# A hybrid attention and recurrence layer: the forget sums and the memory's second tile one step earlier, and eight block copies ahead of panel 12

## The chip, the cores and the metric

The kernel runs on one core of one Trainium2 chip. The metric is the device time of one execution in microseconds. Three runs of the kernel before took 755.61, 753.70 and 755.33 us, with a median of 755.33.

## What is computed

One layer for 512 tokens of width 1024, in float32: a combined input projection, forgetting attention with 8 heads of 64 (FoX), a gated linear recurrence with 4 heads (HGRN2), an output projection, cross attention to 256 memory tokens, a squared-ReLU MLP of width 4096 and a final norm. Cut to what bears on the change:

```python
hn = rmsnorm(h, norm_mix_g)
fq, fk, fv, ff, gq, gf, gi, gg = split(hn @ w_in)
log_f = log_sigmoid(ff + fox_f_bias)
F = cumsum(log_f, axis=-1)                       # per head over the tokens
s = einsum('bhqd,bhkd->bhqk', q, k) / 8 + F[:, :, :, None] - F[:, :, None, :]
fox = softmax(where(causal, s, -inf)) @ v
rec = hgrn2_chunkwise(gq, gf, gi, lb)            # state S_t = diag(f_t) S_{t-1} + k_t i_t^T
rec = rmsnorm(rec, hgrn_norm_g) * silu(gg)
h = h + concat(fox, rec) @ w_out
mem_n = rmsnorm(mem, norm_mem_g)
h = h + memory_cross_attention(rmsnorm(h, norm_x_g), mem_n, w_xq, w_xkv, w_xo)
u = rmsnorm(h, norm_ff_g) @ w1
h = h + square(relu(u)) @ w2
return rmsnorm(h, final_norm_g)
```

## The kernel before

All products run on PE in float32 of high and low parts: an operand is split into hi (ACT, `wh...`, L184) and lo = raw − hi (DVE, `wl...`, L188), and three matmuls make a product. The weights stream through as panels 0 to 28 or so; a panel's raw tiles `wr...` are loaded on SP's queue, in two halves a and b (L210). Panels 5 to 11 are the seven products of a block scheme (`product_unit`, L264), in which block sums take the place of single blocks. Some of their operands are made by loads on POOL's queue that accumulate into the tile: `third_sum` (L256, four tiles `wrs`, used by the splits wh9, wl9) and `fourth_sum` (L260, wrs6a and wrs6b, used by wh11, wl11). Panels 12, 13 and 15 are attention queries and keys of head pairs, 14 attention values, 16 and more belong to the memory and the projections behind.

The MLP far behind uses the same scheme with block sums that are made in DRAM beforehand. For each sum a **block copy** (`first`, L496: 512 KB of a weight block from DRAM to DRAM scratch, tiles `wsu` and `wsd`) goes out on SP's queue, and later an accumulating load on POOL's queue adds the other block (L507). The copies wait in a list, `copies`. `load_unit` takes so many of them behind each part of a panel as the table `COPIES` says for the panel's number (L215), and the projection panels take more from 24 on. `keep_in_program_order` fixes their place on SP's queue. There are 45 copies in all.

Around the change PE runs the recurrence's output in four steps c = 0 to 3 of 128 tokens each (L1064 and on), and fills the time between them with matmuls of the attention's projections (`fill`). A step:
- PE makes po; ACT squares it (`hj`, L1093); POOL turns the sums into the norm's factor (`hr...e`, L435, and `hr`, L438); DVE scales it (`rec`, L1097).
- PE transposes `rec` of the step before (`pr`, L1046); ACT and DVE write it as `mx_hi` (L1047) and `mx_lo` (L1048).

Two pieces of preparation for what follows hang on these steps by the numbers `MT, NF = 3, 2`:
- At c == NF, `fox_rows(0)` (L1023) broadcasts the forget sums F of the first two heads from DRAM (`Fd`) to all 128 partitions: two tiles `nF` of 256 KB, loaded on POOL's queue (L1026).
- At c == MT, `load_mem(1)` (L1030) loads the memory's second tile of 128 tokens (`mt`, POOL's queue, L1032) and normalises it: two squares on ACT (`m1j`, L445), their sum on DVE (`m1m`, L446), the factor on POOL (`m1re`, L435, `m1r`, L438), the scaling on DVE (`mt`, L448).

Behind the recurrence comes the attention of the first pair. POOL makes the biases from nF (`bi`, L1165, with the causal mask, L1166); PE the scores `ps` (L1174); DVE adds the bias and takes the maximum (L1185); ACT the exponential (L1187); DVE the reciprocal `dn` and the product (L1188, L1189). PE then transposes the probabilities (`pt`, L1201), which DVE and ACT copy (`pts`). A scheduler orders each engine's instructions ahead of time by priorities; each engine works through its own list in that order.

Of the kernel before, what the change touches and what calls it, by code (L numbers as in the profile page):

```python
# [30 lines left out]
GF = 5  # L31
WARM, WARM2 = 7, 4
P1, P2, P3, P4, PW = 20, 20, 20, 10, -20
MT, NF = 3, 2
F1, F2, F3, F4, B1 = 1.6, 3.2, 1.5, 1.0, 2.0

FX = (4.4, 4.4, 5.4, 5.4), (3.3, 3.9, 4.5, 5.1)
# [1 line left out]
NEG = -3.0e38  # L39
SEVEN = (1, 2, 3, 4, 5, 6, 7)  # L40
RAWS, HB, LOADS = 5, 4, 8
COPIES = {12: 2, 14: 3, 17: 2, 19: 1, 20: 0, 24: 1}
PACE = (178.0, 4.7), (301.0, 11.5)


# [1 line left out]
def emit(  # L47
# [61 lines left out]
    def t2(name, dt=F32, shape=(S,)):  # L109
        return t2p.tile([P] + list(shape), dt, tag="t2", name=name)  # L110
# [12 lines left out]
    def sc(name, shape=(S,)):  # L123
        return scp.tile([P] + list(shape), F32, tag="sc", name=name)
# [24 lines left out]
    def block0(rc):  # L149
        r, c = int(rc[0]), int(rc[1])  # L150
        return w_in[r * S : (r + 1) * S, 2568 + c * S : 2568 + (c + 1) * S].rearrange("(k p) n -> p k n", p=P)
# [19 lines left out]
    copies, copied = deque(), set()  # L171
    UW, UK = WT + FH, KC // 2

    def new_parts(shape, name):
        pad = [P, UK * (UW + FH)]
        hi = whp.tile([P, shape[0] * shape[1]], R, tag="wh", name=f"wh{name}", padded_shape=pad)
        lo = wlp.tile([P, shape[0] * shape[1]], R, tag="wl", name=f"wl{name}", padded_shape=pad)
        return [t.rearrange("p (k n) -> p k n", k=shape[0]) for t in (hi, lo)]

    def split_of(hi, lo, raw):  # L180
        def split(what="hl"):
            at = None
            if "h" in what:
                at = ac.activation(hi, raw, AF.Copy)  # L184
            if "v" in what:
                ve.tensor_copy(hi, raw)
            if "l" in what:
                at_lo = ve.tensor_tensor(lo, raw, f(hi), ALU.subtract)  # L188
                return at or at_lo
            return at  # L190

        return split

    def load_unit(name, spec, ks, parts=1, between=None):
# [12 lines left out]
        for q in range(parts):  # L207
# [5 lines left out]
            if between is not None:  # L213
                between(q)
            for _ in range(next((n for at, n in reversed(COPIES.items()) if len(stream) >= at), 0)):  # L215
                if copies:
# [4 lines left out]
    def load_next(parts=2, between=None):  # L221

        i = len(stream)
        if i >= len(specs):
            return []
        if callable(specs[i]):
            return specs[i]()
        units, splits = [], []
        uk = specs[i][0][1].shape[1] // 2
        for n in range(2):  # L230
            note = None if between is None else (lambda q, n=n: between(n * parts // 2 + q))
            unit, some = load_unit(f"{i}{'ab'[n]}", specs[i], slice(n * uk, (n + 1) * uk), parts // 2, note)
            units.append(unit)
            splits += some
        stream.append(tuple([u[x] for u in units] for x in range(2)))
        return splits
# [3 lines left out]
    def load_block(name, rc, tiles):  # L240
        raw0[name] = tiles
        for u, t in enumerate(tiles):
            tc.keep_in_program_order(nc.sync.dma_start(t, block0(rc)[:, 2 * u : 2 * u + 2, :]))
# [20 lines left out]
    def product_unit(name):  # L264
        parts = [new_parts([2, S], f"{len(stream)}{u}") for u in "ab"]
        stream.append(tuple([u[x] for u in parts] for x in range(2)))
        if name in "13":
            pad = [P, UK * UW]
            tiles = [wrp.tile([P, 2 * S], F32, tag="wr", name=f"wr0{name}{u}", padded_shape=pad) for u in "ab"]
            load_block(name, "00" if name == "1" else "11", [t.rearrange("p (k n) -> p k n", k=2) for t in tiles])  # L270
        if name == "1":
            for k in range(4):
                t = q2p.tile([P, S], F32, tag="q2", name=f"wrs7{k}")
                tc.keep_in_program_order(nc.sync.dma_start(t, block0("01")[:, k, :]))
                sums7.append(t)
        jobs = []
        for u in range(2):
            hi, lo = parts[u]
            if name == "7":
                jobs += [split_of(hi[:, k, :], lo[:, k, :], sums7[2 * u + k]) for k in range(2)]  # L280
                continue
            raw = raw0[{"2": "5", "4": "6"}.get(name, name)][u]
            jobs.append(split_of(hi, lo, raw))
        if name == "3":
            jobs.append(fourth_sum)
        if name == "3":
            jobs.append(lambda: load_block("5", "10", raw0["5"]))
        return jobs
# [60 lines left out]
    def ahead(n):  # L349

        return tc.high_priority(offset=n) if n else nullcontext()
# [217 lines left out]
    def x_park(c):  # L569
        part, dst = c // 2, park[:, c, :]  # L570
        if c % 2 == 0:
            ac.activation(dst, xps[c], AF.Copy)
        else:
            ve.tensor_copy(dst, xps[c])
        parked.add(c)
        if c ^ 1 in parked:
            gp.dma_start(xTd[part], park[:, 2 * part : 2 * part + 2, :])

    def x_sq(tb):
        junk = s4([D], f"x0j{tb}")  # L580
        if tb < 2:
            ac.activation(junk, xt[:, tb, :], AF.Square, scale=1.0 / 32.0, accum_out=ms0[:, tb : tb + 1])
        else:
            ve.tensor_tensor_reduce(out=junk, in0=xt[:, tb, :], in1=xt[:, tb, :], scale=1.0 / D, scalar=0.0, op0=ALU.mult, op1=ALU.add, accum_out=ms0[:, tb : tb + 1])
# [4 lines left out]
    with tc.manual_schedule(engines={mybir.EngineType.Activation, mybir.EngineType.DVE}):  # L589
# [26 lines left out]
        def l_soft():  # L616
# [12 lines left out]
        jobs = (  # L629
            (first[1],),  # L630
            (lambda: x_park(0), lambda: x_park(1), first[2]),
            (first[3], lambda: second.extend(load_next())),
            (lambda: x_sq(0), lambda: x_park(3)),
            (lambda: x_park(2), lambda: second[0]("h"), lambda: x_sq(2)),
            (lambda: x_sq(1), lambda: second[0]("l"), lambda: x_sq(3)),
            (lambda: second[1]("hl"), l_soft),
            (),
# [47 lines left out]
        def qt_(h):  # L685
            return (Mv, Sa)[h % 2][h // 2][:, h % 2, :]
# [336 lines left out]
    def fox_rows(p):  # L1023
        for h in (2 * p, 2 * p + 1):
            fF[h] = t2(f"nF{h}")
            gp.dma_start(fF[h], Fd[h, :].partition_broadcast(P))  # L1026
# [37 lines left out]
    for c in range(NT):  # L1064
        cs = slice(c * P, (c + 1) * P)
        it = iv[c // 2][:, c % 2, :].rearrange("p (h v) -> p h v", v=P)
        gt = gg[c // 2][:, c % 2, :].rearrange("p (h v) -> p h v", v=P)
        po = sc(f"po{c}", (4, P))
        for h in range(4):
            te.matmul(po[:, h, :], Ag[h // 2][:, (h % 2) * 4 + c, :], it[:, h, :], start=True, stop=c == 0)  # L1070
            if c > 0:
                te.matmul(po[:, h, :], qt_(h)[:, cs], St[:, h, :], start=False, stop=True)
        if c < NT - 1:
            pst = sc(f"pst{c}", (4, P))
            for h in range(4):
                te.matmul(pst[:, h, :], kts[c][:, h, :], it[:, h, :], start=True, stop=True)
            if c < NT - 2:
                k_T(c + 1)
            with ahead(P2):
                Sn = t2(f"S{c}", F32, (4, P))  # L1080
                if c == 0:
                    ve.tensor_copy(Sn, pst)
                else:
                    for h in range(4):
                        ve.scalar_tensor_tensor(
                            Sn[:, h, :], St[:, h, :], Fg[h // 2][:, h % 2, c * P : c * P + 1], pst[:, h, :], op0=ALU.mult, op1=ALU.add
                        )
                St = Sn
        with ahead(P1):
            hs = sm(4, f"hs{c}")  # L1090
            for h in range(4):
                j = t2(f"hj{c}{h}", F32, (P,))
                ac.activation(j, po[:, h, :], AF.Square, scale=128.0 ** -0.5, accum_out=hs[:, h : h + 1])  # L1093
            hr = rstd_of(hs, 4, f"hr{c}")
            rec = t2(f"rec{c}", F32, (4, P))
            for h in range(4):
                ve.scalar_tensor_tensor(rec[:, h, :], po[:, h, :], hr[:, h : h + 1], gt[:, h, :], op0=ALU.mult, op1=ALU.mult)  # L1097
        fill.run(H1)
        if c == NT - 2:
            fill.until("proj0")  # L1100
        if c == MT:
            load_mem(1)
        if c == NF:
            fox_rows(0)
        if pending is not None:
            to_mix(*pending)
        pending = (c, rec)
        fill.run(H2)
# [839 lines left out]
    with tc.manual_schedule(engines={mybir.EngineType.Activation, mybir.EngineType.DVE}):  # L1948
        c = KC - 1
# [105 lines left out]
```

## Time and profile before

| | value |
|---|---|
| runs | 755.61, 753.70, 755.33 us (median 755.33) |
| the profiled execution's own time | 754.02 us |
| its span | 752.2 us |
| mean granted clock of PE | 0.993 |
| PE busy | 740.2 us (98%) |
| DVE busy | 565.5 us (75%) |
| ACT busy | 460.4 us (61%) |
| POOL busy | 212.5 us (28%) |
| DMA moved | 159.22 MB, mean 212 GB/s |

The span is the time between the first and the last instruction in the trace; the execution's own time lies 1.8 us over it. All times in what follows are counted from the start of the span. In a row of the timeline stand the start, the busy time, the engine, the line, the operation, out<-in, the shapes, and in brackets how long the engine had idled before, and for what. A "q" behind an engine's name means the queue of its DMA issues. The chapters on stretches (windows) give busy time per engine, then PE's granted clock, the mean busy share of the 16 DMA engines and GB/s.

### The profile page before, as it was taken

To read this page: it belongs to the slowest core of one execution; us is meant where nothing else is said; L and a number is where in the kernel's file an instruction comes from. 1 tells how busy PE (TensorE), PEld (TensorE's weight loads), DVE (VectorE), ACT (ScalarE), POOL (GpSimd) and SP (SyncE) were. 2 spreads that over 40 slices of the span, in tenths; PEclk is the share of its full clock that TensorE was granted. 3 is DMA by queue.
4 is the path that set the end of the run, shared out by engine and by line. 5 is a ranking of instruction groups with operands and counts; after the bars stand their busy time and mean duration, and the time that the engine had idled before them with its cause. 6 is when DMAs were issued, how large, how long until landed. Compare 5 with 4: busy or idle time off the path is not lost.

```text
span 752.2 us, 12313 instructions
## 1 busy us (share of the span) xinstructions
PE 740.2 (98%) x4557; PEld 646.4 (86%) x4557; DVE 565.5 (75%) x892; ACT 460.4 (61%) x769; POOL 212.5 (28%) x290
## 2 busy tenths in 40 slices
PE   9999999979999999999999999999999999999996
PEld 6889888878888888888888899898989899999985
DVE  5876996656788856645555798978788787878796
ACT  5965776545666642334444589666576757574864
POOL 8225842332433227721111212111111111100034
PEclk9999999989999999999999999999999999999999
DMA  7787859948856799987579799998989898977452
GB/s 228 261 215 196 195 142 341 341 146 291 275 201 213 259 273 220 186 169 135 115 167 203 106 251 229 247 224 244 229 214 240 222 246 211 245 195 233 132 112 112
DMA packets 111919, 159.22 MB, mean 212 GB/s; under 512 B 6338, under 2 KB 74219, under 8 KB 111859
## 3 DMA queue, kind: packets, MB, share of 16 engines
q1 hardware_dynamic: 85490, 114.62, 46.9%
q0 software_dynamic: 26208, 43.54, 33.0%
q8 instruction: 36, 0.59, 0.3%
q10 hardware_dynamic: 160, 0.27, 0.1%
q14 instruction: 25, 0.20, 0.1%
HBM read 153.15 MB, written 51.40 MB: 272 GB/s over the span
## 4 chain that ended last, share of the span: by engine, by line
PE 88%; DMA 4%; ACT 3%; DVE 2%; issue 1%; POOL 1%; POOLq 0%; DVEq 0%; SPq 0%; ACTq 0%
PE uU L1630 4%; PE uU L1632 4%; PE uU L1631 4%; PE U L1789 4%; PE U L1788 4%; PE U L1790 4%; PE uY L1632 2%; PE uY L1631 2%; PE uY L1630 2%; PE xk L1144 2%; PE xq L314 2%; PE wo L314 2%; PE xq L315 2%; PE xw L314 2%; PE xq L316 2%; PE xw L316 2%
## 5 line engine op out<-in xcount | busy, mean ns | idle before, releaser
L188 DVE TENSOR_TENSOR wlu<-wru,whu 128x1024 fp32r<-128x1024 f32 x53 | 63.8, 1221 | 25.6 <-ACT whu L184 25.6
L184 ACT ACTIVATE whu<-wru 128x1024 fp32r<-128x1024 f32 x53 | 55.6, 1058 | 40.9 <-PE U L1790 16.8
L188 DVE TENSOR_TENSOR wld<-wrd,whd 128x1024 fp32r<-128x1024 f32 x56 | 68.2, 1221 | 13.8 <-ACT whd L184 13.5
L184 ACT ACTIVATE whd<-wrd 128x1024 fp32r<-128x1024 f32 x56 | 59.0, 1054 | 15.2 <-PE uU L1631 7.1
L1788 PE MATMUL U<-whd,hb 128*128 128x512 f32 x120 | 46.8, 390 | 0.0
L1789 PE MATMUL U<-wld,hb 128*128 128x512 f32 x120 | 46.8, 390 | 0.0
L1790 PE MATMUL U<-whd,hb 128*128 128x512 f32 x120 | 46.7, 389 | 0.0
L1165 POOL TENSOR_SCALAR bi<-nF,Ft 128x128 f32<-128x128 f32 (+3 forms) x32 | 20.7, 654 | 63.5 <-PE pt L1201 27.6
L507 POOL DMA_DIRECT2D wsd<-in_w_dram x16 | 17.8, 1114 | 68.2 <-PE xw L316 16.6
L1630 PE MATMUL uU<-xs_hi,whu 128*128 128x256 f32 x128 | 36.3, 284 | 0.0
L1632 PE MATMUL uU<-x_hi,wlu 128*128 128x256 f32 x128 | 36.2, 283 | 0.0
L1630 PE MATMUL uY<-xs_hi,whu 128*128 128x256 f32 x128 | 36.2, 283 | 0.0
L1631 PE MATMUL uY<-xs_lo,whu 128*128 128x256 f32 x128 | 36.2, 283 | 0.0
L1632 PE MATMUL uY<-xs_hi,wlu 128*128 128x256 f32 x128 | 36.2, 283 | 0.0
L1632 PE MATMUL uU<-xs_hi,wlu 128*128 128x256 f32 x128 | 36.2, 283 | 0.0
L1631 PE MATMUL uU<-x_lo,whu 128*128 128x256 f32 x128 | 36.2, 283 | 0.0
L1631 PE MATMUL uU<-xs_lo,whu 128*128 128x256 f32 x128 | 36.2, 283 | 0.0
L1630 PE MATMUL uU<-x_hi,whu 128*128 128x256 f32 x128 | 36.2, 283 | 0.0
L1526 POOL DMA_DIRECT2D wrd<-in_w_dram x8 | 9.8, 1223 | 86.6 <-DVE wld L188 59.6
L507 POOL DMA_DIRECT2D wsu<-in_w_dram x14 | 16.9, 1210 | 44.3 <-PE xq L316 14.5
L1187 ACT ACTIVATE bi<-bi,mx 128x128 f32<-128x128 f32 (+3 forms) x32 | 17.9, 559 | 18.4 <-DVE mx L1185 17.4
L1790 PEld LDWEIGHTS U<-whd,hb 128*128 128x128 f32 x120 | 22.5, 188 | 4.7
(1012 smaller groups left out, 2650.9 us busy)
## 6 DMA issues: line engine op xcount, KB each, us to landing
wru<-in_w_dram SPq DMA_DIRECT2D x25, 512.0 KB, 6.7
wsd<-in_w_dram SPq DMA_DIRECT2D x24, 512.0 KB, 8.5
wrd<-in_w_dram SPq DMA_DIRECT2D x24, 512.0 KB, 4.1
wrd<-wsd SPq DMA_DIRECT2D x24, 512.0 KB, 5.3
wsu<-in_w_dram SPq DMA_DIRECT2D x21, 512.0 KB, 7.0
wru<-wsu SPq DMA_DIRECT2D x21, 512.0 KB, 4.8
wsd<-in_w_dram POOLq DMA_DIRECT2D x16, 512.0 KB, 7.9
wsu<-in_w_dram POOLq DMA_DIRECT2D x14, 512.0 KB, 7.2
```

What stands on the lines that cost most here:

```text
L184: at = ac.activation(hi, raw, AF.Copy)
L188: at_lo = ve.tensor_tensor(lo, raw, f(hi), ALU.subtract)
L314: te.matmul(ps, wh, hi, start=n_ == 0 and not begun, stop=False)
L316: at = te.matmul(ps, wl, hi, start=False, stop=k == order[-1])
L507: yield gp.dma_start(wsum[kind, g, name], src, accum_op=ALU.add, **more)
L1165: gp.tensor_scalar(bi[:, 0:n], fF[h][:, 0:n], -1.0, Ft[:, tb, h : h + 1], op0=ALU.mult, op1=ALU.add)
L1630: te.matmul(ps[:, i, :], whi[:, k, ws], xh[:, k, :], start=begin, stop=False, skip_group_check=True)
L1631: te.matmul(ps[:, i, :], whi[:, k, ws], xl[:, k, :], start=False, stop=False, skip_group_check=True)
L1632: at = te.matmul(ps[:, i, :], wlo[:, k, ws], xh[:, k, :], start=False, stop=k == UK - 1, skip_group_check=True)
L1788: te.matmul(ps, hi, whi[:, k, :], start=begin, stop=False, skip_group_check=True)
L1789: te.matmul(ps, hi, wlo[:, k, :], start=False, stop=False, skip_group_check=True)
L1790: at = te.matmul(ps, lo, whi[:, k, :], start=False, stop=k == 1, skip_group_check=True)
```

## The change

Two numbers, one table and two lines change:

```diff
-MT, NF = 3, 2
+MT, NF = 2, 1
...
-COPIES = {12: 2, 14: 3, 17: 2, 19: 1, 20: 0, 24: 1}
+COPIES = {12: 2, 19: 1, 20: 0, 24: 1}
...
         if name == "3":
             jobs.append(fourth_sum)
+        if name in "24":
+            jobs += [lambda: tc.keep_in_program_order(copies.popleft()())] * 4
         if name == "3":
             jobs.append(lambda: load_block("5", "10", raw0["5"]))
...
+        if c == NF:
+            fox_rows(0)
         if c == MT:
             load_mem(1)
-        if c == NF:
-            fox_rows(0)
```

So `fox_rows(0)` stands in step c = 1 and not 2, `load_mem(1)` in step 2 and not 3; and two of the product units take four copies each, eight together. Panels 14 to 16 then take two copies per part instead of three, and the copies beside the projection panels end two earlier; the number of copies is the same. PE's order does not change.

POOL's order before, from the second step's norm (hr1) on; `kl` is cleared for the second pair's keys:

```order
L435 TENSOR_SCALAR hr1e<-hs_1602 128x4
L438 TENSOR_TENSOR hr_1613<-hr1e,mhalf 128x4
L993 MEMSET kl_1790 64x512 x2
L435 TENSOR_SCALAR hr2e<-hs_1687 128x4
L438 TENSOR_TENSOR hr_1698<-hr2e,mhalf 128x4
L1026 DMA nF_1708<-Fd 128x512
L1026 DMA nF_1710<-Fd 128x512
L435 TENSOR_SCALAR hr3e<-hs_1737 128x4
L438 TENSOR_TENSOR hr_1748<-hr3e,mhalf 128x4
L1165 TENSOR_SCALAR bi_1797<-nF_1708,Ft 128x128
L1165 TENSOR_SCALAR bi_1802<-nF_1710,Ft 128x128
```

The same place of POOL in the changed kernel, whose lines are two further down:

```order
L437 TENSOR_SCALAR hr1e<-hs_1610 128x4
L440 TENSOR_TENSOR hr_1621<-hr1e,mhalf 128x4
L1028 DMA nF_1631<-Fd 128x512
L1028 DMA nF_1633<-Fd 128x512
L995 MEMSET kl_1796 64x512 x2
L437 TENSOR_SCALAR hr2e<-hs_1697 128x4
L440 TENSOR_TENSOR hr_1708<-hr2e,mhalf 128x4
L437 TENSOR_SCALAR m1re<-m1m 128x1
L440 TENSOR_TENSOR m1r<-m1re,mhalf 128x1
L437 TENSOR_SCALAR hr3e<-hs_1756 128x4
L440 TENSOR_TENSOR hr_1767<-hr3e,mhalf 128x4
L1167 TENSOR_SCALAR bi_1803<-nF_1631,Ft 128x128
```

The broadcasts moved from behind hr2 to right behind hr1, and the memory tile's factor (m1re, m1r) to ahead of hr3e; before, it stood eight rows behind hr3, after the masked biases of two steps. The load of the second memory tile itself has the same place and the same wait as before.

DVE's order before, from the third step's `rec` on; `qk` and `q` are the second pair's queries:

```order
L1097 SCALAR_TENSOR_TENSOR rec_1700<-po_1668,hr_1698,gg_917 128x128 x4
L1048 SCALAR_TENSOR_TENSOR mx_lo<-pr_1712,gv,mx_hi 128x4x128
L1097 SCALAR_TENSOR_TENSOR rec_1750<-po_1728,hr_1748,gg_917 128x128 x4
L985 SCALAR_TENSOR_TENSOR qk_1663<-pq_1664,rbc 128x512
L446 TENSOR_TENSOR m1m<-m1m 128x1
L1048 SCALAR_TENSOR_TENSOR mx_lo<-pr_1774,gv,mx_hi 128x4x128
L448 TENSOR_SCALAR mt_1761<-mt_1761,m1r 128x1024
L989 TENSOR_TENSOR q_1661<-qk_1663,q_1661 64x512
```

The same place of DVE in the changed kernel:

```order
L1099 SCALAR_TENSOR_TENSOR rec_1710<-po_1678,hr_1708,gg_917 128x128 x4
L1050 SCALAR_TENSOR_TENSOR mx_lo<-pr_1731,gv,mx_hi 128x4x128
L448 TENSOR_TENSOR m1m<-m1m 128x1
L450 TENSOR_SCALAR mt_1718<-mt_1718,m1r 128x1024
L1099 SCALAR_TENSOR_TENSOR rec_1769<-po_1747,hr_1767,gg_917 128x128 x4
L1050 SCALAR_TENSOR_TENSOR mx_lo<-pr_1780,gv,mx_hi 128x4x128
L987 SCALAR_TENSOR_TENSOR qk_1673<-pq_1674,rbc 128x512
L991 TENSOR_TENSOR q_1671<-qk_1673,q_1671 64x512
```

The memory tile's sum and scaling (m1m, mt) moved ahead of the last `rec`, and qk behind the next mx_lo; ACT's two squares m1j moved in the same way from behind the last step's four hj to ahead of them. Behind q the order is the same.

SP's queue in the changed kernel, from the last load of a product unit on:

```order
L243 DMA wrs5b<-in_w_in_dram 128x2x512
L499 DMA wsu_194<-in_w_dram 512x1x256
L499 DMA wsd_197<-in_w_dram 256x1x512
L499 DMA wsu_195<-in_w_dram 512x1x256
L499 DMA wsd_198<-in_w_dram 256x1x512
L499 DMA wsu_196<-in_w_dram 512x1x256
L499 DMA wsd_199<-in_w_dram 256x1x512
L499 DMA wsu_200<-in_w_dram 512x1x256
L499 DMA wsd_203<-in_w_dram 256x1x512
L210 DMA wr12a<-in_w_in_dram 128x4x128 x2
L499 DMA wsu_201<-in_w_dram 512x1x256
L499 DMA wsd_204<-in_w_dram 256x1x512
```

Before, wr12a followed directly on wrs5b, and the first copy on wr12a. Now eight copies stand between them; the two copies behind wr12a, wr12b and each later part of panels 12 and 13 remain.

## The prediction

> **What bounds the kernel now.** I read the page's busy times first, then what TensorE (PE) waits for over the whole span, then the timeline and the granted clock around the longest of those waits.
>
> ```profile
> PE 740.2 (98%) x4557; PEld 646.4 (86%) x4557; DVE 565.5 (75%) x892; ACT 460.4 (61%) x769; POOL 212.5 (28%) x290
> ```
> ```profile
> PE pt L1201 <- DVE bi L1189: 4.3, 2, 4.0
> PE warm L426 <- DVE ones L430: 1.3, 1, 1.3
> PE dg L865 <- DVE Ac L868: 0.2, 1, 0.2
> ```
> PE is busy for 98% of the span, so an edit on another engine counts only where it ends a wait of PE or starts one, or changes PE's clock. In the rows of waits stand the total, the times and the longest. After the warm-up PE waits 0.2 at L865 and 4.3 at the first transposes of the forgetting attention (pt, L1201), which need VectorE's normalised probabilities.
>
> ```profile
> 159.15 0.28 PE L329 MATMUL fv<-wh14b,hn_lo 128*128 128x256 f32 x1
> 163.41 0.45 PE L1201 MATMUL pt<-ident,bi 128*128 128x128 f32 x1 [3.98 <-DVE bi L1189]
> 164.14 0.45 PE L1201 MATMUL pt<-ident,bi 128*128 128x128 f32 x1 [0.29 <-DVE bi L1189]
> 172.08 0.60 PE L1201 MATMUL pt<-ident,bi 128*128 128x128 f32 x4
> ```
> ```profile
> 159.40:163.40 4.00, 0.03 (x1) 0.03 (x1) 3.80 (x9) 0.91 (x4) 0.15 (x1) 0.75 0.44 85
> 163.40:168.20 4.80, 4.50 (x20) 4.25 (x21) 3.29 (x9) 3.25 (x8) 0.00 (x0) 0.50 0.97 343
> 168.20:172.24 4.04, 4.04 (x36) 4.04 (x35) 1.93 (x8) 2.15 (x7) 0.00 (x0) 0.99 1.05 346
> ```
> In the windows the first pair of numbers is PE's busy time; the last three are granted clock, DMA share and GB/s. PE ends its work at 159.43, idles 3.98 and 0.29, and then works at clock 0.50 until 168.2. So the place costs more than its waits.
>
> Followed back, the wait leads to two broadcasts on GpSimd (POOL):
>
> ```profile
> 136.32 1.03 POOL L438 TENSOR_TENSOR hr<-hr1e,mhalf 128x4 f32<-128x4 f32 x1
> 144.96 1.16 POOL L1026 DMA_DIRECT2D nF<-Fd  x2
> 152.64 0.38 POOL L1165 TENSOR_SCALAR bi<-nF,Ft 128x128 f32<-128x128 f32 x1 [4.53 <-DMA nF<-Fd]
> 155.74 0.19 POOL L435 TENSOR_SCALAR m1re<-m1m 128x1 f32<-128x1 f32 x1
> 156.01 0.55 POOL L438 TENSOR_TENSOR m1r<-m1re,mhalf 128x1 f32<-128x1 f32 x1
> ```
> ```profile
> 156.60 1.09 DVE L448 TENSOR_SCALAR mt<-mt,m1r 128x1024 f32<-128x1024 f32 x1 [6.00 <-POOL m1r L438]
> 157.72 1.67 DVE L989 TENSOR_TENSOR q<-qk,q 64x512 fp32r<-64x512 f32 x2
> 163.71 0.29 DVE L1189 TENSOR_SCALAR bi<-bi,dn 128x128 f32<-128x128 f32 x1
> ```
> The broadcasts are issued from 144.96, POOL's first bias stands 4.53 for them until 152.64, and behind the biases of two steps stands the tiny norm of the second memory tile (m1re, m1r). VectorE (DVE) idles 6.00 for m1r, scales the tile (mt), and only then goes through q, wl15a, mx_lo and the softmax, whose last step ends at 164.00. From q's start to there it takes 6.28.
>
> **The change part by part.** *First, the broadcasts.* They now stand right behind the second hr, which ends at 136.32 + 1.03 = 137.35, so 7.6 ahead of 144.96. Their landing:
>
> ```profile
> mt<-in_mem_dram POOLq DMA_DIRECT2D x1, 512.0 KB, 6.6
> nF<-Fd POOLq DMA_DIRECT2D x2, 256.0 KB, 7.6
> ```
> With 7.6 again they are there at about 146, before POOL is through with the last hr. The two issues stand ahead of the clearing of kl on POOL, whose user comes later; hr2e waits for ScalarE (ACT) until 143.71 anyway. I cost this at nothing; its cover is POOL's idle time ahead of hr2e.
>
> *Second, the norm of the second tile*, now ahead of the last recurrence step on ACT, POOL and DVE. Its load is issued no earlier and not later, since it waits for PE:
>
> ```profile
> 134.15 0.65 POOL L1032 DMA_DIRECT2D mt<-in_mem_dram  x1 [3.24 <-PE pst L1076]
> ```
> ```profile
> 145.57 0.28 ACT L1093 ACTIVATE hj<-po 128x128 f32<-128x128 f32 x1 [1.44 <-PE po L1072]
> 149.90 1.29 ACT L988 ACTIVATE q<-qk 64x512 fp32r<-64x512 f32 x2 [1.39 <-DVE qk L985]
> ```
> ```profile
> 146.08 0.74 DVE L1048 SCALAR_TENSOR_TENSOR mx_lo<-pr,gv,mx_hi 128x512 fp32r<-128x512 f32 x1
> 148.14 1.13 DVE L1097 SCALAR_TENSOR_TENSOR rec<-po,hr,gg 128x128 f32<-128x128 f32 x4 [1.32 <-POOL hr L438]
> 149.19 0.68 DVE L985 SCALAR_TENSOR_TENSOR qk<-pq,rbc 128x512 f32<-128x512 f32 x1
> 163.91 0.68 DVE L997 TENSOR_TENSOR qk<-pk,rbc 128x512 f32<-128x512 f32 x1
> 169.86 0.36 DVE L1189 TENSOR_SCALAR bi<-bi,dn 128x256 f32<-128x256 f32 x1
> ```
> ```profile
> 151.26 0.60 PE L1046 MATMUL pr<-ident,rec 128*128 128x128 f32 x4
> ```
> Load: 134.15 + 6.6 = 140.8. ACT's two squares fall into the 1.44 in which it waited ahead of hj, so nothing there. DVE's sum m1m comes behind mx_lo, at 146.82; from m1re to mt took 0.86 (155.74 to 156.60), so mt starts at 146.82 + 0.15 (the sum, an estimate) + 0.86 = 147.83 and ends by 148.92. On POOL hr3e and hr3 come behind m1r, so hr3 ends 1.0 later, and rec, which waited for it, starts at about 149.1, not 148.14. PE takes its transposes at 151.26, rec ends 150.25: margin 1.0. That is the cover of the move; without it every later step slips by the excess.
>
> Then, shifted by 1.0: mx_lo 150.15, qk 150.8, ACT's q (0.71 behind qk) 151.5, DVE's q at about 152.2 when the first half is there. Adding the 6.28 of before, the softmax ends at **158.5**, before PE's 159.43: margin 0.9, and the wait goes. The next step: from qk at 163.91 to 169.86 + 0.36 = 170.22 DVE took 6.31; from 158.4 that is 164.7. PE would reach that step's transposes at 159.43 + half of 4.51 + 3.88 = 165.57 (4.51 is the half-clock stretch without the 0.29; 3.88 is 168.20 to 172.08). Margin 0.8. No other wait of PE lies behind, and all PE work behind moves up together.
>
> The gain: 3.98 + 0.29 of waits, and half of 4.80 − 0.29 = 4.51 us, so 2.26. **Sum 6.53.**
>
> A page speaks on this stall. In the Trainium skill, "TensorE: Matmul & The Clock Gate", section "What's actually happening", the clock halves after an idle window of about 3.4 us and is full again after about 3.4 us of sustained work; by it the recovery would be worth an estimated 1.7 and the sum 6.0. The trace agrees on the half clock after 3.98 of idle, but shows 4.8 us at 0.50, so the measured stretch decides.
>
> *Third, the copies.* Eight block copies of 512 KB, 4.19 MB, go out behind wrs5b and ahead of wr12a on SP's queue. What DMA does there now, how long accumulating loads took, and who waits first behind:
>
> ```profile
> 77.00:87.00 10.00, 10.00 (x72) 8.14 (x71) 8.99 (x20) 8.61 (x14) 7.58 (x9) 1.00 0.82 169
> 102.00:112.00 10.00, 10.00 (x74) 8.44 (x73) 9.91 (x22) 7.89 (x12) 4.30 (x12) 1.00 0.19 69
> ```
> ```profile
> wrs<-in_w_in_dram POOLq DMA_DIRECT2D x4, 256.0 KB, 6.3
> wrs6b<-in_w_in_dram POOLq DMA_DIRECT2D x1, 512.0 KB, 12.0
> ```
> ```profile
> 121.88 1.07 ACT L184 ACTIVATE wh13b<-wr13b 128x1024 fp32r<-128x1024 f32 x1 [0.91 <-DMA wr13b<-in_w_in_dram]
> 122.85 1.06 ACT L1016 ACTIVATE A<-pa 128x512 f32<-128x512 f32 x2
> ```
> ```profile
> 90.27 1.13 ACT L184 ACTIVATE wh9a<-wrs 128x512 fp32r<-128x512 f32 x2
> ```
> ```profile
> 96.79 0.39 PE L841 MATMUL gU<-wh9a,mx_hi 128*128 128x512 f32 x1
> 125.35 0.72 PE L1070 MATMUL po<-iv,A 128*128 128x128 f32 x5
> ```
> At 346 GB/s the copies need 12.1 us of all engines. Idle shares offer 1.8 (77 to 87) and 8.1 (102 to 112), 9.9 together; so at 112, about when panel 13's loads join the queue, 0 to 2.2 us of copies stand ahead of them. ACT already waits 0.91 for wr13b; behind it come the copies A, ending at 123.91, which PE takes at 125.35: 1.44 of slack. So the bounds for PE are 0 and 2.2 − 1.44 = 0.8; I take 0, since a later user hides most of what is late. The four accumulating loads ahead of wh9 could go from 6.3 toward 12.0, 5.7 later. ACT takes the first two at 90.27 without waiting, PE the result at 96.79; with 1.13 on ACT and about as much on DVE (an estimate) 4.2 are free, so the bounds for PE are 0 and 1.5, and I take 0 again, since ACT's start at 90.27 was not set by the load. On the other side, six copies fewer stand between the loads of panels 14 to 16 and two fewer beside w_out's panels. PE waited for none of those loads, so that gains nothing.
>
> A rule speaks against this part: the Trainium skill, "DMA: Bandwidth & Descriptors", section "Queues, rings and completion order", has each DMA engine go round-robin between queues, a packet at a time, so a full SP queue would halve what POOL's accumulating loads get. The row of 12.0 beside 6.3 agrees in direction, and a doubling of 6.3 would give an estimated 12.6, hardly past the bound I use.
>
> **Rivals.**
> 1. *A rest of the wait, or the last recurrence step late.* All three margins are 0.8 to 1.0 and rest on shifted rows. If mt lands after 12.0 instead of 6.6, at 146.15, ACT's hj, the norm and everything behind come 1 to 2 later, and PE waits 0.5 to 2, too short for the half clock by what the rows show. For it: thin margins. Against: DVE idles now where the work goes. Time 754.02 − 6.53 + 0.5 to 2, so 748.0 to 749.5, on the median's basis up to 751.
> 2. *The copies collide mildly:* PE waits 1.5 to 4 between 96 and 126 for a split of wh9 or for the A copies. For it: DMA is full from 87 to 102 already. Against: 8.1 us of idle DMA follow. Time 749 to 752.5.
> 3. *The copies are not absorbed, slower than before.* Place: the wait of ACT for wr13b and, behind it, PE's po at 125.35. Price: lateness less 1.44, and once PE idles some 4 us, 2.3 more for the half clock. It decides when that sum passes 6.5, that is with wr13b 5.7 us late, 2.0 of the 4.19 MB still queued at 112. For it: the eight copies all stand ahead of panel 12's loads, in one row. Against: idle shares hold 9.9 of 12.1 us. Time 756 to 760.
> 4. *The change doesn't do it:* another releaser, wh15a or wh15b on ACT, holds DVE's chain as long as m1r did. ACT had ended wh15b at 154.81 in the order before, hence little for it. Time 753 to 755.5.
>
> ```profile
> 153.75 1.06 ACT L184 ACTIVATE wh15b<-wr15b 128x1024 fp32r<-128x1024 f32 x1 [0.90 <-PE pk L315]
> ```
>
> **How the numbers follow.** The sum against the profiled execution is 754.02 − 6.53 = 747.5; that run stands 1.31 below the median of the runs shown, 755.33, against which it is 748.8. I predict **748.4**, between the two and nearer to the median. The forecast has a chance of 0.60 with a range of its own of 746.5 to 749.5; rival 1 has 0.15, rival 2 0.10, rival 3 0.09, rival 4 0.06. Low end: the forecast against the fastest of the runs, 753.7 − 6.5 = 747.2, less some noise, 746.5. High end: 753.0 takes in rivals 1 and 2. A measurement of this kernel tells about 0.3% from no change, 2.3 us. Faster by more: forecast, rivals 1 and 2 but for a small part, 0.82; within: most of rival 4 and small parts, 0.08; slower: rival 3 and a rest, 0.10.
>
> **What would show it.** Right: no wait of PE at pt and a clock of 1.00 through the stretch after the last fv of that step; mt on DVE before the last rec; POOL's first bias not waiting for nF; rec ending within 1 us of PE's transposes; DMA share near 1 from 102 to 111; wh13b waiting not much over 0.91. Wrong: PE waiting at lv, gU or po between 90 and 126, ACT's wh13b waiting over 2.4, or pt still waiting for L1189 with DVE idle behind a split of panel 15.

## The result and the profile after

The changed kernel takes 748.68 us (748.24 to 749.36, four runs) against 755.10 for the kernel before (753.70 to 755.61): a ratio of 0.9919, with a 95% interval of 0.9902 to 0.9936; the medians differ by 6.4 us. Its profiled execution took 748.24. Predicted were 748.4, in a range of 746.5 to 753.0. Among the kernels further on, one run each of two of them lay far above their other runs (2181.59 with the copies alone, 808.62 with twelve copies) and is left out of their medians and ratios.

First the page's line of busy times and what PE waits for over the whole span, in the changed kernel. Its line numbers are two higher than those of before.

```profile
PE 738.6 (99%) x4557; PEld 645.3 (86%) x4557; DVE 566.6 (76%) x892; ACT 460.4 (62%) x769; POOL 213.4 (29%) x290
```
```profile
PE warm L428 <- DVE ones L432: 1.3, 1, 1.3
PE dg L867 <- ACT fv L793: 0.4, 1, 0.4
```

The wait at pt is gone, and nothing has taken its place in the list. PE's timeline at the same point, and the two windows in which it stood and then worked at half clock before:

```profile
152.08 0.60 PE L1048 MATMUL pr<-ident,rec 128*128 128x128 f32 x4
...
159.94 0.28 PE L331 MATMUL fv<-wh14b,hn_lo 128*128 128x256 f32 x1
160.06 0.38 PE L1203 MATMUL pt<-ident,bi 128*128 128x128 f32 x2
...
166.23 0.60 PE L1203 MATMUL pt<-ident,bi 128*128 128x128 f32 x4
```
```profile
159.40:163.40 4.00, 4.00 (x36) 4.00 (x36) 2.56 (x6) 2.76 (x7) 0.00 (x0) 1.00 0.95 325
163.40:168.20 4.80, 4.80 (x41) 4.80 (x41) 3.45 (x13) 4.29 (x11) 1.49 (x3) 1.00 0.83 309
```

PE goes from fv into pt without a gap, at a clock of 1.00. The next step's transposes start at 166.23 and not at 172.08: 5.85 earlier, although PE came to pt 0.63 later in this execution (160.06 against 159.43). From there to the end of the span both executions need the same time: 746.5 − 166.23 = 580.3 after, 752.2 − 172.08 = 580.1 before. So the whole gain was made at this one place.

POOL and DVE around it, in the changed kernel:

```profile
138.15 1.17 POOL L1028 DMA_DIRECT2D nF<-Fd  x2
...
148.10 0.55 POOL L440 TENSOR_TENSOR m1r<-m1re,mhalf 128x1 f32<-128x1 f32 x1
148.74 0.76 POOL L437 TENSOR_SCALAR hr3e<-hs 128x4 f32<-128x4 f32 x1
149.57 1.02 POOL L440 TENSOR_TENSOR hr<-hr3e,mhalf 128x4 f32<-128x4 f32 x1
150.60 0.74 POOL L1167 TENSOR_SCALAR bi<-nF,Ft 128x128 f32<-128x128 f32 x2
```
```profile
148.69 0.76 DVE L450 TENSOR_SCALAR mt<-mt,m1r 128x1024 f32<-128x1024 f32 x1 [0.94 <-POOL m1r L440]
150.63 1.13 DVE L1099 SCALAR_TENSOR_TENSOR rec<-po,hr,gg 128x128 f32<-128x128 f32 x4 [1.19 <-POOL hr L440]
...
159.66 0.29 DVE L1191 TENSOR_SCALAR bi<-bi,dn 128x128 f32<-128x128 f32 x1
...
165.74 0.35 DVE L1191 TENSOR_SCALAR bi<-bi,dn 128x256 f32<-128x256 f32 x1
```

The broadcasts leave at 138.15, 6.8 earlier than before, and POOL's first bias waits for nothing. m1r ends at 148.65, which was 156.56 before, and the softmax ends at 159.95, 0.1 ahead of PE's first transpose.

DMA, in two windows and two rows of issues (KB each, median us to landing), and the wait of ACT that stood for the copies' rival:

```profile
77.00:87.00 10.00, 10.00 (x72) 8.13 (x71) 8.98 (x19) 9.13 (x16) 8.78 (x10) 1.00 1.00 316
...
102.00:112.00 10.00, 10.00 (x74) 8.42 (x73) 9.41 (x22) 7.64 (x13) 4.50 (x11) 1.00 1.00 338
```
```profile
wr12a<-in_w_in_dram SPq DMA_DIRECT2D x2, 256.0 KB, 18.0
...
wr13a<-in_w_in_dram SPq DMA_DIRECT2D x2, 256.0 KB, 4.8
```
```profile
122.69 1.06 ACT L184 ACTIVATE wh13b<-wr13b 128x1024 fp32r<-128x1024 f32 x1 [0.98 <-DMA wr13b<-in_w_in_dram]
```

The copies filled the idle stretches to the brim: from 102 to 112 the share went from 0.19 to 1.00. Panel 12's load landed after 18.0 us instead of 4.1, still in time, and panel 13's took no longer than before (4.8, where it was 5.2).

### The profile page after: what moved, and what is told of

It reads as the page before. It is cut to its first block, busy times and chain, and to the rows that moved or that the text cites. A ratio compares the mean times of both kernels' runs of the same rounds, so it can differ in the third digit from the quotient of the medians.

```text
span 746.5 us, 12316 instructions
## 1 busy us (share of the span) xinstructions
PE 738.6 (99%) x4557; PEld 645.3 (86%) x4557; DVE 566.6 (76%) x892; ACT 460.4 (62%) x769; POOL 213.4 (29%) x290
## 4 chain that ended last, share of the span: by engine, by line
PE 90%; DMA 3%; DVE 2%; ACT 2%; issue 1%; POOL 0%; POOLq 0%; DVEq 0%; SPq 0%; ACTq 0%
PE uU L1632 4%; PE uU L1634 4%; PE uU L1633 4%; PE U L1790 3%; PE U L1791 3%; PE U L1792 3%; PE uY L1634 2%; PE uY L1633 2%; PE uY L1632 2%; PE xk L1146 2%; PE xq L316 2%; PE wo L316 2%; PE xq L317 2%; PE xq L318 2%; PE xw L318 2%; PE xw L317 2%
## 5 line engine op out<-in xcount | busy, mean ns | idle before, releaser
L1318 ACT ACTIVATE x_hi<-hT,gv 128x512 fp32r<-128x512 f32 x15 | 10.7, 714 | 25.8 <-DVE hT L1317 25.8
```

## The experiments

Theory A was that the wait came from one chain on POOL, in which the memory tile's factor stood behind biases that waited for the broadcasts. Its rivals were that the copies bring part of the gain (B), and that both moves are needed (C). The kernel before ran again beside each group of kernels: its medians were 755.09 beside the first four, 754.41 beside the next four and 755.07 beside the last two. The ratios below are to these runs, and not quotients of medians.

**Only the broadcasts move.**

```diff
-MT, NF = 3, 2
+MT, NF = 3, 1
```
(`fox_rows` stands ahead of `load_mem` in the loop, as in the changed kernel; the table of copies is that of before.)

> Only the broadcasts of the forget sums move (NF = 1); the memory's second tile and the copies stay as before. Theory A (the wait came from the tile's factor m1r standing on POOL behind biases that waited for the broadcasts): the broadcasts land at about 146, POOL goes through the biases of two steps without waiting and m1r ends at about 152.9, mt on VectorE at about 154; TensorE still waits about 1 us at pt, too short for the half clock; 5 to 6 us below before, about 749.5. Theory B (the copies taken out of the stretch 112 to 150 give part of the gain): 3 to 4 below before. Theory C (both moves are needed): the wait stays over 3 us, within 1.5 of before.

Measured: 747.86 (747.56 to 748.35), ratio 0.9906 (0.9891 to 0.9921). POOL's and DVE's rows of this kernel:

```profile
151.44 0.55 POOL L438 TENSOR_TENSOR m1r<-m1re,mhalf 128x1 f32<-128x1 f32 x1
```
```profile
152.03 1.09 DVE L448 TENSOR_SCALAR mt<-mt,m1r 128x1024 f32<-128x1024 f32 x1 [1.14 <-POOL m1r L438]
...
159.14 0.29 DVE L1189 TENSOR_SCALAR bi<-bi,dn 128x128 f32<-128x128 f32 x1
```

m1r comes 0.9 earlier than expected (it ends at 151.99); the softmax ends at 159.43, and PE reaches pt at 159.56. The whole wait is gone with this move alone, and the time is 7.2 below before. Theory A holds in kind; the rest of 1 us at pt that it expected isn't there.

**Only the memory's second tile moves.**

```diff
-MT, NF = 3, 2
+MT, NF = 2, 2
```
(Here too `fox_rows` stands ahead of `load_mem`, and the table of copies is that of before.)

> Only the memory's second tile moves (MT = 2); the broadcasts stay in the third step and the copies as before. Theory A: m1r is through before POOL waits for the broadcasts, and the first biases, masked by about 154.8, are still in time for VectorE at about 156, so no wait at pt: 6 to 6.7 below before, 748.5 to 749. Theory B: 3 to 4 below before. Theory C: the wait stays over 3 us, within 1.5 of before.

Measured: 747.93 (747.45 to 748.76), ratio 0.9907 (0.9891 to 0.9923). The rows of POOL and DVE in this kernel, around the broadcasts and at the end of the softmax:

```profile
147.24 0.57 POOL L438 TENSOR_TENSOR m1r<-m1re,mhalf 128x1 f32<-128x1 f32 x1
...
152.85 1.68 POOL L1165 TENSOR_SCALAR bi<-nF,Ft 128x128 f32<-128x128 f32 x2 [3.10 <-DMA nF<-Fd]
```
```profile
158.98 0.29 DVE L1189 TENSOR_SCALAR bi<-bi,dn 128x128 f32<-128x128 f32 x1
```

POOL still waits 3.10 for the broadcasts, and it costs nothing: m1r is through before. The softmax ends at 159.27, and PE takes pt at 159.27 without a wait, so with nothing to spare. The chain ended by the factor, not by the broadcasts, so it can be cut at either end, and theory C falls.

**Both moves without the copies.**

> Both moves, the copies as before. Theory A: the whole gain, 6 to 6.7 below before, the same as the changed kernel within 0.5. Theory B: 2 or more above the changed kernel. Theory C: as theory A.

Measured: 748.00 (747.69 to 748.63), ratio 0.9910 (0.9895 to 0.9925). PE waits for nothing but its start and 0.2 at L865, as before. So the two moves together bring no more than one of them, and the copies are not needed for it.

**Only the copies.**

> Only the eight copies move; MT, NF = 3, 2 as before. Theory A and C: no change within 0.7 of before, and the wait of 4 us at pt with the half clock behind it stays; the broadcasts land perhaps 1 to 2 us earlier, which shortens the wait by at most as much. Theory B: 2 to 3 us below before.

Measured: 752.36 (nine runs, 750.43 to 753.25), ratio 0.9957 (0.9942 to 0.9971). PE's waits, and ACT's waits ahead of the new one:

```profile
PE pt L1203 <- DVE bi L1191: 2.4, 2, 2.0
PE pk L1055 <- ACT A L1018: 1.7, 1, 1.7
```
```profile
119.43 1.06 ACT L184 ACTIVATE wh13a<-wr13a 128x1024 fp32r<-128x1024 f32 x1 [0.84 <-DMA wr13a<-in_w_in_dram]
...
124.17 1.06 ACT L184 ACTIVATE wh13b<-wr13b 128x1024 fp32r<-128x1024 f32 x1 [1.88 <-DMA wr13b<-in_w_in_dram]
```
```profile
165.00:168.20 3.20, 3.20 (x29) 3.20 (x28) 1.92 (x4) 3.10 (x6) 0.00 (x0) 1.00 1.04 379
```

Here theory A was wrong: it gave no change, and the time fell by 2.7, as theory B had it. The wait at pt shrank from 4.3 to 2.4, with a clock of 1.00 behind it, since the broadcasts landed after 5.0 instead of 7.6. And the collision that the prediction held as a rival is there: ACT waits 0.84 for the first half of panel 13, where it waited for none before, and 1.88 for the second, 0.97 more than before; PE waits 1.7 for the A copies behind them. PE's place there in the kernel before:

```profile
123.12 0.40 PE L316 MATMUL pq<-hn_hi,wl12b 128*128 128x512 f32 x1
123.48 0.33 PE L1053 MATMUL pk<-ident,sta 128*128 128x128 f32 x1
```

pk's tile comes from the same pool of two buffers as the two tiles pa (`tr`, L126), so pk stands until ACT has made the first A copy out of pa. That copy ended at 123.43 (0.58 after 122.85), and pk began 0.05 behind it. So ACT had no slack here. The same order of SP's queue had shown no such wait in the changed kernel's profile, so its size differs between executions.

**The changed kernel and the moves alone, side by side.**

> The changed kernel once more, beside the next kernel on the same chip. Theory D (the eight copies fill the last idle DMA time before panel 13's loads, so that these are late in some executions and not in others, by 0 to 1.7 us of TensorE's time): 0.2 to 1.2 above the kernel with the two moves alone. Theory A' (the copies cost and bring nothing): the same within 0.2.

> The two moves without the copies once more, as the other side of the pair: 747.5 to 748.3 by both theories, with no wait of TensorE beyond the 1.5 us of its start.

Measured on one chip: 748.17 (748.00 to 749.20) with the copies, 747.77 (747.48 to 748.30) without. The profile of the changed kernel, an execution of 749.20, has this row among PE's waits, and the one without has none of the kind:

```profile
PE pk L1055 <- ACT A L1018: 0.5, 1, 0.5
```

Four profiles of kernels with the eight copies thus show 0, 0.5, 1.7 and, in the last kernel below, 0.4 at that place. The 0.4 between the medians lies within the spread of the runs, so theory D's sign is likely and its size is not settled.

**More copies at that place.** Twelve and sixteen instead of eight:

```diff
-            jobs += [lambda: tc.keep_in_program_order(copies.popleft()())] * 4
+            jobs += [lambda: tc.keep_in_program_order(copies.popleft()())] * 6
```
(and `* 8`)

> The changed kernel with twelve copies instead of eight ahead of panel 12; four fewer copies later. Theory D: DMA has no idle time left between 77 and 112, so the four copies more (2.1 MB, 6 us at 340 GB/s) make panel 12's and 13's loads up to 6 us late; with 1.4 of slack TensorE stands 3 to 5 us before 126, and the half clock may add 2: 751.5 to 755. Theory E (a queue that is full costs no more than the 1.7 us seen once): within 2 of the changed kernel.

> The changed kernel with sixteen copies ahead of panel 12; eight fewer later. Theory D: 4.2 MB more than the changed kernel, 12 us at 340 GB/s, so TensorE stands 9 to 11 us before 126 and works at half clock behind it for 2 more: 758 to 762, above the kernel before. Theory E: within 3 of the changed kernel.

Measured: 753.68 (nine runs, 752.25 to 754.37; 0.9983, 0.9973 to 0.9994) with twelve, and 762.20 (1.0093, 1.0075 to 1.0111) with sixteen. PE's wait and ACT's two in the kernel of twelve:

```profile
PE pa L1017 <- ACT wh13a L184: 3.2, 1, 3.2
```
```profile
113.13 1.06 ACT L184 ACTIVATE wh12a<-wr12a 128x1024 fp32r<-128x1024 f32 x1 [3.50 <-DMA wr12a<-in_w_in_dram]
...
119.19 1.06 ACT L184 ACTIVATE wh12b<-wr12b 128x1024 fp32r<-128x1024 f32 x1 [5.00 <-PE gU L845]
```
```profile
124.30:127.30 3.00, 2.94 (x12) 2.58 (x13) 2.92 (x5) 1.87 (x6) 2.62 (x5) 0.53 1.09 330
```

The same of sixteen:

```profile
PE pa L1017 <- DVE A L959: 4.3, 1, 4.3
PE pq L316 <- ACT wh12a L184: 3.7, 1, 3.7
```
```profile
122.31 1.06 ACT L184 ACTIVATE wh12a<-wr12a 128x1024 fp32r<-128x1024 f32 x1 [12.10 <-DMA wr12a<-in_w_in_dram]
```
```profile
125.00:131.00 6.00, 3.04 (x7) 1.83 (x6) 3.03 (x7) 3.78 (x6) 0.00 (x0) 0.50 1.08 355
131.00:137.00 6.00, 4.67 (x16) 3.98 (x17) 4.91 (x10) 4.53 (x9) 4.11 (x7) 0.52 1.01 329
```

With four copies more ACT waits 3.5 for panel 12's first half, and starts the second half at 119.19, where the changed kernel did at 111.61. The profile puts this second wait down to PE, but in the changed kernel ACT didn't need that product of PE for it; SP issued the second half's loads from 108.84 to 111.86, and they landed after 7.9, so at about 119, and it is likely the load that ends the wait. The A copies behind it come late, and PE waits 3.2 with half clock after it. With eight copies more ACT waits 12.1 and PE twice, 3.7 and 4.3, at half clock until about 137. Theory D holds and E falls, though for sixteen D had the waits longer (9 to 11) and the half clock shorter than they were. Of the three numbers tried eight is the only one that fits, and sixteen is slower than the kernel before with the stall at pt gone. With twelve and sixteen it is panel 12's loads, right behind the copies, that are late first; with eight it was panel 13's.

**The changed table without the early copies.** In the kernel before:

```diff
-COPIES = {12: 2, 14: 3, 17: 2, 19: 1, 20: 0, 24: 1}
+COPIES = {12: 2, 19: 1, 20: 0, 24: 1}
```

> The kernel before with the changed table of copies alone: panels 14 to 16 take two copies per part and not three, nothing goes out ahead of panel 12, and the copies left over come beside the projection panels from 24 on. Theory F (the copies alone gained 2.7 since fewer transfers stand beside the broadcasts, which then land after 5.0 instead of 7.6): the broadcasts land after 5 to 6, the wait at pt falls to about 2 with full clock behind it, and nothing is paid ahead of panel 13: 3 to 4.5 below before. Theory G (the gain came from the early place of the eight): no change within 0.7 of before.

Measured: 751.74 (749.91 to 752.46), ratio 0.9950 (0.9937 to 0.9963). The DMA row of the broadcasts, PE at pt, and its clock behind:

```profile
nF<-Fd POOLq DMA_DIRECT2D x2, 256.0 KB, 5.5
```
```profile
162.11 0.30 PE L1201 MATMUL pt<-ident,bi 128*128 128x128 f32 x1 [2.34 <-DVE bi L1189]
162.85 0.45 PE L1201 MATMUL pt<-ident,bi 128*128 128x128 f32 x1 [0.43 <-DVE bi L1189]
```
```profile
163.00:165.50 2.50, 2.50 (x13) 2.50 (x13) 1.20 (x3) 2.10 (x4) 0.00 (x0) 0.50 0.99 350
```

Theory F holds for the time, 3.3 below before, and for the wait; the full clock that it expected behind the wait isn't there. It is the copies taken away beside the broadcasts that let these land 2.1 sooner after their issue and shorten the wait, and not the early place of the eight. Copies and moves thus worked on the same wait; once the moves have removed it, the copies have nothing left to give.

**The scaling of the memory tile behind the last rec.** In the changed kernel a dependency puts mt's scaling on DVE behind rec (the lines that hand the scaling out of `norm_rows` are left out here):

```diff
+    scaled = scale1()
+    sync = mybir.DependencyInfo(mybir.DependencyClass.Sync, mybir.DependencyReason.DATA)
+    tc.add_manual_dep(scaled.ins, at_rec.ins.name, sync, reason="scale")
```

> The changed kernel with the scaling of the memory's second tile on VectorE made to wait for the last rec; the same work otherwise. Theory H (GpSimd's hr3e took 0.76 instead of 0.19 because VectorE's scaling of mt began 0.05 before it and kept it from its operands): hr3e takes 0.19 again, rec starts 0.5 to 0.6 earlier against TensorE's transposes pr, and the softmax ends 0.2 to 0.6 earlier against pt. Theory I (hr3e is slow for another reason): it stays over 0.6. By both the time is that of the changed kernel within 0.4, as TensorE waits for none of it.

Measured: 748.29 (747.75 to 748.97), ratio 0.9908 (0.9895 to 0.9921). PE's wait, and POOL's and DVE's rows of this kernel:

```profile
PE pk L1059 <- ACT A L1021: 0.4, 1, 0.4
```
```profile
148.32 0.19 POOL L437 TENSOR_SCALAR hr3e<-hs 128x4 f32<-128x4 f32 x1
```
```profile
149.65 1.13 DVE L1103 SCALAR_TENSOR_TENSOR rec<-po,hr,gg 128x128 f32<-128x128 f32 x4 [2.33 <-POOL hr L440]
...
151.95 0.89 DVE L450 TENSOR_SCALAR mt<-mt,m1r 128x1024 f32<-128x1024 f32 x1
...
159.04 0.29 DVE L1195 TENSOR_SCALAR bi<-bi,dn 128x128 f32<-128x128 f32 x1
```

hr3e takes 0.19 again, and theory H holds. rec starts 2.0 ahead of PE's transposes (at 151.66), where the changed kernel had 1.45. The softmax ends at 159.33, and PE takes pt at 159.66: 0.3 ahead of it, where the changed kernel had 0.1. It gains only 0.2, as mt's scaling, 0.89, now stands between rec and q on DVE. The time is that of the changed kernel; PE waits 0.4 for the A copies behind the eight block copies, and for none of what this edit moved.

## Why the prediction was right

- **The stall and its half clock, 6.53.** Right in kind and size. The wait at pt and the half clock behind it are gone; the medians differ by 6.4, and between the profiled executions 5.85 came from this place after 0.63 of a later arrival, so 6.48. The moves alone, in four kernels without the copies, gained 6.6 to 7.2. That 748.4 lies within 0.3 of the result is in part luck: it was set between two bases 1.3 apart, and the runs of the changed kernel spread by 1.1.
- **The moves cost nothing.** Right, but with much less room than the working said. The three margins were given as 0.8 to 1.0. Measured: rec ended at 150.63 + 1.13 = 151.76 and PE took it at 152.08, so 0.3; the softmax ended 0.1 ahead of pt; the next step's ended at 165.74 + 0.35 = 166.09, 0.1 ahead of PE's 166.23. The step that was mis-sized is "hr3e and hr3 come behind m1r, so hr3 ends 1.0 later": POOL's hr3e took 0.76 instead of 0.19, since it ran into DVE's scaling of mt, which began 0.05 before it. That added 0.6, and the last kernel above shows it: hr3e takes 0.75 or 0.76 in all seven profiles in which it starts just behind the scaling, and 0.19 in the other five. Had the margin been missed, rival 1 would have cost as much as the miss.
- **What the working took for granted** was that the two moves act as one. The runs show that either alone removes the whole wait. The prediction followed the chain of before to its start, the broadcasts, where a cut at its last link, m1r, does the same; it didn't ask what each move is worth alone.
- **The copies at nothing.** Nearly right in size, but not for the reason given. The slack of 1.44 was read from PE's po at 125.35, the wrong user: PE's pk at L1053 stands for the first A copy and began 0.05 behind it, at 123.48, so the slack was nothing. With it the bounds for PE would have been 0 and 2.2, and not 0 and 0.8, and rival 3 would have had nothing to take off its lateness. Measured were 0, 0.4, 0.5 and 1.7 in four profiles, the last outside the bound given, and 0.4 between medians of runs with and without the copies. What ACT was late reached PE in full: 0.48 more of waiting for wr13b in the changed kernel's second profile gave 0.5 at pk. That the term came out near 0 is so in part luck. The account of idle DMA time held: the stretch from 102 to 112 was filled to 1.00, and what was left over was small. The collision came where it was looked for, behind panel 13's loads. The other bound, 0 to 1.5 for the accumulating loads, held: PE waited for none of them.
- **The copies taken away later, at no gain.** Right in the changed kernel. But the reason given looked at the loads of the panels beside them alone, for which PE didn't wait, and not at the broadcasts, which landed after 5.5 instead of 7.6 once those copies were away. In the kernel before, this landing was on the path, and there the changed table alone gains 3.3.
- **The accumulating loads.** They took 9.1 (wrs) in the changed kernel where they had taken 6.3, so not twice as long, and inside the bound of 12.0 that was used. The round-robin between queues of the Trainium skill, "DMA: Bandwidth & Descriptors", section "Queues, rings and completion order", had given an estimated 12.6; the trace agrees with it in direction only. The row of issues:

```profile
wrs<-in_w_in_dram POOLq DMA_DIRECT2D x4, 256.0 KB, 9.1
```

## What to carry to other kernels

Where a wait is fed by a chain of several waits on one engine, ask of every link what cutting it alone would do: here two edits and a third, each meant to help, worked on the same 6.5 us, and one would have been enough. Idle DMA time is a stock to be counted: moved transfers are nearly free until they fill it (here eight copies, 0 to 1.7), and what goes past that is late for whoever stands behind them in the queue (four copies more cost 5.5). Before a slack is set against lateness, look for the first user of everything that the late engine sets free, buffers too: the 1.44 was taken from a later one. Leave a margin for the engines' own collisions where two of them get new neighbours, as 0.6 on POOL used up most of what was counted as room here.

## What the runs showed of the hardware

- **A short instruction on POOL waits out DVE's scaling.** hr3e on 4 columns took 0.76 where mt's scaling on DVE ran from 148.69 to 149.45, and 0.19 where it was moved away. The Trainium skill, "SBUF — State Buffer", section "SBUF: two separate sides", says that GpSimd and DVE, in DVE's two-port modes or with two inputs in SBUF, share one pair of ports as an exclusive lock, so that the one that comes second stands until the first is done. hr3e ended at 149.50, 0.05 after the scaling: the trace agrees; in which mode the scaling ran, no row tells. The order may decide which of the two stands: in the four kernels in which a bias of POOL began 0.03 or 0.04 ahead of the scaling, as in the kernel before, it was the scaling that took longer, 1.09 or 1.10 and not 0.76.
- **The half clock follows shorter waits than one might think.** Waits of PE and the clock behind them: 3.98 and 0.50 in the kernel before, 3.20 and 0.53 with twelve copies, 2.34 (with 0.43 behind it) and 0.50 for about 2.5 us in the kernel of the changed table, but 2.02 (with 0.43) and 1.00 in that of the copies alone. In the kernel before, the clock was down well ahead of the end of the wait: the mean of 0.71 below puts the step from 1.00 to 0.50 at about 161.4, an estimate, and so 2.0 after PE had stopped at 159.43. The Trainium skill, "TensorE: Matmul & The Clock Gate", section "What's actually happening", names an idle window of about 3.4 us; these runs show the half clock already after waits of 3.20 and 2.34. What tells 2.34 from 2.02 isn't settled by two cases.

```profile
161.00:162.00 1.00, 0.00 (x0) 0.00 (x0) 1.00 (x4) 0.36 (x2) 0.00 (x0) 0.71 0.16 33
```
- **Copies in a row hold SP itself.** In the changed kernel the last of the eight copies took SP 4.55 to issue, and the two loads of panel 12's first half behind it 10.59, where before these two took 1.03. That the queue was full is a likely reason; no row shows how full it was.

```profile
87.21 10.59 SPq L210 DMA_DIRECT2D wr12a<-in_w_in_dram  x2
```
